# Where the low halves of weights are made: an adding DMA for the first weights of a sub-layer, VectorE for all 256-column chunks

## The chip, the cores and the metric

One core of one Trainium2 chip runs the whole program. The metric is the device time in microseconds (us) of one execution; lower is better. Engines are named as in the profile: PE is TensorE (matrix products, with PEld for its weight loads), DVE is VectorE, ACT is ScalarE, POOL is GpSimd, SP is SyncE, which here only issues DMA transfers.

## The reference

Two layers act on 512 latent tokens and 256 context tokens of width 1024, in float32. The even layer mixes by attention, the odd one by a short convolution; the context is dropped after the first layer's attention.

```python
def modulate(x, g, shift, scale):
    return rmsnorm(x, g) * (1 + scale) + shift

def swiglu(x, w_gate, w_up, w_down):
    return (jax.nn.silu(x @ w_gate) * (x @ w_up)) @ w_down

def macaron_ffn(xs, g, shift, scale, gate, w_gate, w_up, w_down):
    return xs + 0.5 * gate * swiglu(modulate(xs, g, shift, scale), w_gate, w_up, w_down)
...
    for i in range(DEPTH):
        ...
        x_lat = macaron_ffn(x_lat, norm_g[i, 0], m[0], m[1], m[2], ...)
        ...
        xn = modulate(x_lat, norm_g[i, 1], m[3], m[4])
        # even: xn @ w_in, neighbourhood and differential attention, @ w_out
        # odd:  xn @ w_in, three-tap convolution, @ w_out
        x_lat = x_lat + m[5] * y
        x_lat = macaron_ffn(x_lat, norm_g[i, 2], m[6], m[7], m[8], ...)
    return rmsnorm(x_lat, final_g)
```

## The kernel before

Each float32 product is made of three products of a shorter format: a weight is split into a high half `wh` and a low half `wl`, an activation into `xh` and `xl`, and `mm3` (L140) adds `wh·xh`, `wh·xl` and `wl·xh` in one accumulator. A weight tile is 128x1024 and serves as eight blocks of 128x128; a matmul streams 256 or 512 columns of tokens.

`load_w` (L109) fetches a weight tile into one of three `raw` buffers by a DMA of SP and splits it into one of three `wh` and one of three `wl` buffers. There are two ways. By default ScalarE copies `raw` to `wh` (L119) and VectorE subtracts (L120). Where `wl_eng[0]` is None, ScalarE writes `-raw` to `wl` (L115), a DMA issued by GpSimd adds `raw` to it (L116), and ScalarE writes `wh` (L117). Before the change only the projections inside attention go the second way: `wl_eng[0]` is set to None behind the first step of the projection stream and reset when the stream is done.

`modulate_chunk` (L287) makes one normalized chunk of 128 channels: a product on VectorE (L290), the high half with the shift on ScalarE (L296), the low half on VectorE (L297). Of chunks with up to 256 columns every third goes another way: ScalarE adds the shift (L292) and copies the high half (L293), and GpSimd subtracts (L294).

A sub-layer's first products are its head: `Head` loads three weights and runs them while the chunks of the first half of the tokens still come in. `transition` (L352) puts the last passes of the sub-layer before, the statistics (`Norm.add`: squares L271 on ScalarE, sums L275 on GpSimd or VectorE, then a matmul with ones, L284), the chunks and the head behind one another. There are five heads: to attention, to the FFN after it (f1), to layer two's first FFN (f2), to the convolution, and to the last FFN (f3). In attention, `proj_v` loads two weights for the first value projection: with the first four blocks of channels TensorE uses one, with the other four the other (L699); beside it the rope of queries and keys runs (shuffle L715, products L716 and L717, sum L718, copies L733 and L758).

The order on each engine is made by a scheduler from the order of the code and its own costs; it reorders instructions within an engine, and the engines wait for one another by semaphores. SP issues its DMAs in that order too, and a load whose buffer is still held keeps the ones behind it waiting.

Of the kernel before, what the change touches and what calls it, by code (L numbers as in the profile page):

```python
# [11 lines left out]
AF = mybir.ActivationFunctionType  # L12
ALU = mybir.AluOpType
# [28 lines left out]
def build(tc, A, out):  # L42

    nc = tc.nc
# [3 lines left out]
    with ExitStack() as es:  # L48
# [9 lines left out]
        def uid(s):  # L58
            cnt[0] += 1
            return f"{s}{cnt[0]}"  # L60
# [9 lines left out]
        def tt_(tag, shape=(P, NT), dtype=F32):  # L70
            return dp.tile(list(shape), dtype, tag=tag, bufs=BUFS[tag], name=uid(tag))

        def tmp(n):

            if n > 256:
                return dt_("pj")
            return dp.tile([P, 256], F32, tag="nh", bufs=BUFS["nh"], name=uid("nh"))
# [17 lines left out]
        wl_eng = [nc.vector]  # L95
# [13 lines left out]
        def load_w(src, n=1024, eng=None):  # L109
            raw = wp.tile([P, 1024], F32, tag="raw", bufs=3, name=uid("raw"))  # L110
            nc.sync.dma_start(raw[:, :n], src)
            hi = wp.tile([P, 1024], F32R, tag="wh", bufs=3, name=uid("wh"))
            lo = wp.tile([P, 1024], F32R, tag="wl", bufs=3, name=uid("wl"))
            if wl_eng[0] is None:
                nc.scalar.activation(lo[:, :n], raw[:, :n], AF.Copy, scale=-1.0)  # L115
                nc.gpsimd.dma_start(lo[:, :n], raw[:, :n], accum_op=ALU.add)  # L116
                nc.scalar.activation(hi[:, :n], raw[:, :n], AF.Copy)  # L117
                return hi, lo
            nc.scalar.activation(hi[:, :n], raw[:, :n], AF.Copy)  # L119
            (eng or wl_eng[0]).tensor_tensor(lo[:, :n], raw[:, :n], hi[:, :n], op=ALU.subtract)  # L120
            return hi, lo
# [135 lines left out]
        class Norm:  # L257


            def __init__(self, n):  # L260
                self.n, self.ss, self.k = n, [None, None], 0
                self.parts = 8
# [24 lines left out]
        def modulate_chunk(k, xk, y, s, b, hi, lo):  # L287
            n = xk.shape[-1]
            t = tmp(n)
            nc.vector.scalar_tensor_tensor(t[:, :n], xk, s[:, k:k + 1], y, op0=ALU.mult, op1=ALU.mult)  # L290
            if n <= 256 and k % 3 == 2:
                nc.scalar.activation(t[:, :n], t[:, :n], AF.Identity, bias=b[:, k:k + 1])  # L292
                nc.scalar.activation(hi, t[:, :n], AF.Copy)  # L293
                nc.gpsimd.tensor_tensor(lo, t[:, :n], hi, op=ALU.subtract)  # L294
                return
            nc.scalar.activation(hi, t[:, :n], AF.Identity, bias=b[:, k:k + 1])  # L296
            nc.vector.scalar_tensor_tensor(lo, t[:, :n], b[:, k:k + 1], hi, op0=ALU.add, op1=ALU.subtract)  # L297

# [5 lines left out]
        class Entry:  # L304
# [12 lines left out]
            def chunks(self, si, ks=range(KD)):  # L317
                l, i, ms, mb = self.key
                s0, s1 = self.segs[si]
                st = "c_ctx" if s0 >= N else "c"  # L320
                if st not in self.s:
                    need(l, ms)
                    need(l, mb)
                    self.s[st] = mod_scale(l, ms, i, st)
                for k in ks:
                    if self.xn[k] is None:
                        self.xn[k] = (tt_("xn", dtype=F32R), tt_("xn", dtype=F32R))
                    hi, lo = self.xn[k]
                    modulate_chunk(k, xseg(k, (s0, s1)), self.y[si], self.s[st], mod[l, mb, st],
                                   hi[:, s0:s1], lo[:, s0:s1])  # L330

        class Head:
# [2 lines left out]

            def __init__(self, units):

                self.w = [load_w(u[0]) for u in units]
                self.units = units

            def run(self, e, si, ks=range(KD), inner=False):
# [400 lines left out]
        def q_out(key, o):  # L742
            q = ((dt_("pj", dtype=F32R), dt_("pj", dtype=F32R)), dt_("pj", dtype=F32R))
            if key[0] == "d":
                q_parts(q, rope(o, 0.125), lambda z: z, None)
            else:
                ends = lambda z: z.rearrange("p (a b) -> p a b", b=64)
                q_parts(q, ends(o)[:, 0:8:7, :], lambda z: ends(z[:, 0:P]), 0.125)
                q_parts(q, o[:, 64:448], lambda z: z[:, P:N], 0.125)
            Q[key] = q  # L750
# [307 lines left out]
        def advance():  # L1058
            try:
                pos[1] += next(stream)  # L1060
            except StopIteration:
                return False
            return True

        advance()
        wl_eng[0] = None
        q_out(("d", 0), head0.o[0][0])
        for o, z in zip(head0.o[1], (SEG_LAT, SEG_CTX)):
            k_out(("d", 0), o, z)
# [24 lines left out]
        for j in range(4):  # L1094
            hi, lo = tt_("xn", dtype=F32R), tt_("xn", dtype=F32R)
# [171 lines left out]
```

## Time and profile before

| | |
|---|---|
| median of 3 runs | 2279.23 us (2277.51 to 2285.79) |
| profiled execution | 2278.66 us, span 2276.8 us |
| PE busy | 2210.0 us, 97% of the span |
| DVE busy | 1350.6 us, 59% |
| ACT busy | 890.5 us, 39% |
| POOL busy | 244.0 us, 11% |
| low halves by VectorE (L120) | 331 |
| low halves by DMA (L116) | 23 |

A row of a group in the profile names line, engine, operation, what is written and read (buffer numbers left out), the shape, the count; then busy time and mean ns of one; then the idle time of the engine just before them and what ended it. A row of the timeline gives start and length in us, the engine, the line, and in square brackets the idle time before it with its cause. In a row of waits stand the total, the count and the longest, in us.

### The profile page before, as it was taken

How to read it: one execution, taken by the hardware profiler on the slowest of the kernel's cores; microseconds unless marked ns; L12 is line 12 of the kernel's file. 1: busy time of each engine (PE TensorE's matmuls, PEld its weight loads, DVE VectorE, ACT ScalarE, POOL GpSimd, SP SyncE). 2: the span in 40 equal slices, each digit the busy share in tenths (PEclk: the TensorE clock that was granted, in tenths of full speed). 3: DMA queues.
4: the chain of work that ended last, by engine and by line, in shares of the span. 5: the costliest groups of instructions: out<-in, count | busy, mean ns of one | idle time of the engine just before them, and what ended most of it. 6: DMA issues, size and time to landing. Idle time of an engine off the chain costs nothing.

```text
span 2276.8 us, 30529 instructions
## 1 busy us (share of the span) xinstructions
PE 2210.0 (97%) x11728; PEld 1880.5 (83%) x11728; DVE 1350.6 (59%) x2388; ACT 890.5 (39%) x1512; POOL 244.0 (11%) x196
## 2 busy tenths in 40 slices
PE   5899999999999999999999999999999999999998
PEld 3688888888888888788888898888888889888887
DVE  8894763534787866775556476555437446443335
ACT  4651431212467887652222253222234224222224
POOL 3551520000221100020000010000001000000001
PEclk9989999999999999999999999999999999999999
DMA  7672443434533434334445444544332322223232
GB/s 240 220 238 83 149 139 107 149 106 130 162 86 77 102 74 113 111 100 159 152 163 178 152 143 157 167 162 159 96 102 93 101 93 92 94 97 98 86 109 74
DMA packets 113306, 291.14 MB, mean 128 GB/s; under 512 B 14468, under 2 KB 18820, under 8 KB 113160
## 3 DMA queue, kind: packets, MB, share of 16 engines
q1 hardware_dynamic: 109848, 277.13, 37.6%
q0 software_dynamic: 3312, 12.06, 2.8%
q8 instruction: 92, 1.51, 0.3%
q14 instruction: 54, 0.44, 0.1%
HBM read 272.88 MB, written 4.19 MB: 122 GB/s over the span
## 4 chain that ended last, share of the span: by engine, by line
PE 85%; DVE 8%; ACT 3%; issue 2%; DMA 1%; POOL 1%; SPq 0%; DVEq 0%; ACTq 0%; POOLq 0%
PE S L145 39%; PE acc L145 38%; PE acc L699 3%; DVE junk L215 1%; DVE wl L120 1%; PE S L768 1%; DVE xn L297 1%; PE S L766 1%; DVE sm L220 1%; DVE nh L290 1%; PE acc L978 1%; PE acc L893 1%; PE acc L1002 1%; POOL P L210 0%; PE acc L878 0%
## 5 line engine op out<-in xcount | busy, mean ns | idle before, releaser
L145 PE MATMUL S<-xn,wh 128*128 128x512 f32 (+1 forms) x3008 | 919.9, 379 | 20.7 <-ACT xn L296 12.7
L119 ACT ACTIVATE wh<-raw 128x1024 fp32r<-128x1024 f32 (+1 forms) x331 | 340.3, 1029 | 1049.9 <-PE acc L145 509.5
L145 PEld LDWEIGHTS S<-xn,wh 128*128 128x128 f32 x3008 | 555.4, 189 | 134.2 <-ACT xn L296 16.2
L120 DVE TENSOR_TENSOR wl<-raw,wh 128x1024 fp32r<-128x1024 f32 (+1 forms) x331 | 397.8, 1203 | 428.4 <-ACT wh L119 425.2
L145 PE MATMUL S<-xn,wl 128*128 128x512 f32 (+1 forms) x1504 | 568.6, 378 | 6.4 <-DVE wl L120 6.2
L145 PE MATMUL acc<-h,wh 128*128 128x512 f32 (+1 forms) x2148 | 531.9, 345 | 3.3 <-DVE x L475 3.2
L145 PE MATMUL acc<-xn,wh 128*128 128x256 f32 (+1 forms) x1664 | 447.7, 330 | 3.3 <-ACT wh L119 1.1
L145 PEld LDWEIGHTS acc<-h,wh 128*128 128x128 f32 x2148 | 363.0, 189 | 58.5 <-issue 3.3
L145 PE MATMUL acc<-h,wl 128*128 128x512 f32 (+1 forms) x1074 | 344.4, 343 | 1.4 <-DVE wl L120 1.4
L145 PEld LDWEIGHTS S<-xn,wl 128*128 128x128 f32 x1504 | 284.7, 189 | 61.0 <-DVE wl L120 8.5
L145 PEld LDWEIGHTS acc<-xn,wh 128*128 128x128 f32 x1664 | 295.3, 191 | 31.5 <-issue 2.5
L145 PE MATMUL acc<-xn,wl 128*128 128x256 f32 (+1 forms) x832 | 271.3, 326 | 2.9 <-DVE wl L120 2.9
L475 DVE SCALAR_TENSOR_TENSOR x<-acc,sm,x 128x512 f32<-128x512 f32 (+1 forms) x216 | 132.2, 629 | 217.2 <-PE acc L145 216.9
L145 PEld LDWEIGHTS acc<-h,wl 128*128 128x128 f32 x1074 | 192.4, 189 | 26.2 <-DVE wl L120 2.0
L215 DVE SCALAR_TENSOR_TENSOR junk<-aux,sc 128x512 bf16<-128x512 f32 x256 | 193.8, 757 | 1.6
L275 POOL TENSOR_TENSOR nh<-nh,nh 128x256 f32<-128x256 f32 x42 | 45.6, 1090 | 1232.9 <-ACT nh L271 898.5
L145 PEld LDWEIGHTS acc<-xn,wl 128*128 128x128 f32 x832 | 159.2, 191 | 16.1 <-DVE wl L120 3.6
L210 POOL TENSOR_TENSOR P<-aux,pv 128x512 f32<-128x512 f32 x64 | 103.4, 1630 | 132.3 <-ACT P L213 68.3
L126 ACT ACTIVATE h<-P 128x512 fp32r<-128x512 f32 (+2 forms) x99 | 62.5, 631 | 108.9 <-DVE P L434 108.8
L127 DVE TENSOR_TENSOR h<-P,h 128x512 fp32r<-128x512 f32 (+2 forms) x99 | 74.0, 747 | 20.1 <-ACT h L126 20.1
L699 PE MATMUL acc<-wh,xn 128*128 128x256 f32 x384 | 78.7, 294 | 0.0
L434 DVE TENSOR_TENSOR P<-P,S 128x512 f32<-128x512 f32 (+1 forms) x91 | 59.8, 657 | 10.4 <-ACT P L433 9.6
(179 smaller groups left out, 1741.8 us busy)
## 6 DMA issues: line engine op xcount, KB each, us to landing
aux<-modw SPq DMA_DIRECT2D x288, 256.0 KB
raw<-wu SPq DMA_DIRECT2D x92, 512.0 KB
raw<-wg SPq DMA_DIRECT2D x91, 512.0 KB
raw<-wd SPq DMA_DIRECT2D x59, 512.0 KB
raw<-wd SPq DMA_DIRECT2D x48, 384.0 KB
raw<-cin SPq DMA_DIRECT2D x24, 512.0 KB
wl<-raw POOLq DMA_DIRECT2D x23, 512.0 KB, 4.8
h<-modw SPq DMA_DIRECT2D x32, 256.0 KB
```

The lines of the kernel that those rows point to most:

```text
L119: nc.scalar.activation(hi[:, :n], raw[:, :n], AF.Copy)
L120: (eng or wl_eng[0]).tensor_tensor(lo[:, :n], raw[:, :n], hi[:, :n], op=ALU.subtract)
L126: nc.scalar.activation(hi, src, AF.Copy)
L127: nc.vector.tensor_tensor(lo, src, hi, op=ALU.subtract)
L145: last_mm[0] = nc.tensor.matmul(o, a, b[:, s0:s1], start=first and ti == 0, stop=last and ti == 2)
L210: nc.gpsimd.tensor_mul(pr, raw, sc[s][h])
L215: i = nc.vector.scalar_tensor_tensor(junk, raw, 1.0, sc[s][h], op0=ALU.mult, op1=ALU.mult, accum_out=a)
L220: nc.vector.scalar_tensor_tensor(o[:, ch:ch + 1], pt[:, 0:1], pt[:, 1:2], modb[:, c:c + 1], op0=ALU.add, op1=ALU.add)
L275: (nc.gpsimd, nc.vector)[i].tensor_add(self.ss[i][:, :n], self.ss[i][:, :n], sq[:, :n])
L434: nc.vector.tensor_mul(sl[:, s0:s1], sl[:, s0:s1], uu)
L475: nc.vector.scalar_tensor_tensor(v, ps, g[:, d:d + 1], v, op0=ALU.mult, op1=ALU.add)
L699: last_mm[0] = nc.tensor.matmul(o, a, b, start=k == 0 and ti == 0, stop=k == KD - 1 and ti == 2)
```

## The change

Weights of the five heads and both weights of the first value projection get their low halves by the adding DMA too (15 + 2 weights). The chunks with up to 256 columns lose their other way, so their 24 subtractions move from GpSimd to VectorE, and ScalarE does one instruction for each instead of two. Lines behind `Head` move by three: L699 becomes L696, L733 becomes L730, and so on; L290 stays, L296 becomes L291 and L297 becomes L292.

```diff
@@ modulate_chunk
             nc.vector.scalar_tensor_tensor(t[:, :n], xk, s[:, k:k + 1], y, op0=ALU.mult, op1=ALU.mult)
-            if n <= 256 and k % 3 == 2:
-                nc.scalar.activation(t[:, :n], t[:, :n], AF.Identity, bias=b[:, k:k + 1])
-                nc.scalar.activation(hi, t[:, :n], AF.Copy)
-                nc.gpsimd.tensor_tensor(lo, t[:, :n], hi, op=ALU.subtract)
-                return
             nc.scalar.activation(hi, t[:, :n], AF.Identity, bias=b[:, k:k + 1])
@@ Head.__init__
+                wl_eng[0] = None
                 self.w = [load_w(u[0]) for u in units]
+                wl_eng[0] = nc.vector
                 self.units = units
@@ attention
+        wl_eng[0] = None
         advance()
-        wl_eng[0] = None
         q_out(("d", 0), head0.o[0][0])
```

The scheduler's order changes around every head. At the f2 head, ScalarE before: `wh` of three weights in turn (L119), between them squares of the statistics (`nh`, L271) and chunks (`xn`, L296).

```order
L296 ACTIVATE xn_12748<-nh_12750,sm_10696 128x256 [waits DVE_49]
L119 ACTIVATE wh_12909<-raw_12907 128x1024 [waits DMAHW7_49,PE_49]
L271 ACTIVATE nh_12769<-x_9629 128x256 [waits DVE_49]
L271 ACTIVATE nh_12785<-x_9630 128x256 [waits DVE_49,Activation_49]
L296 ACTIVATE xn_12788<-nh_12790,sm_10696 128x256 [waits DVE_49]
L119 ACTIVATE wh_12915<-raw_12913 128x1024 [waits DMAHW2_49,PE_49]
L271 ACTIVATE nh_12809<-x_9627 128x256 [waits DVE_49,Pool_49]
L271 ACTIVATE nh_12824<-x_9628 128x256 [waits DVE_49,Activation_49]
L119 ACTIVATE wh_12921<-raw_12919 128x1024 [waits DMAHW3_49,PE_49]
```

And ScalarE now:

```order
L291 ACTIVATE xn_12744<-nh_12746,sm_10692 128x256 [waits DVE_49]
L117 ACTIVATE wh_12903<-raw_12901 128x1024 [waits DMAHW7_49,PE_49]
L271 ACTIVATE nh_12765<-x_9626 128x256 [waits DVE_49]
L271 ACTIVATE nh_12781<-x_9627 128x256 [waits DVE_49,Activation_49]
L115 ACTIVATE wl_12904<-raw_12901 128x1024 [waits DMASW4_49,PE_49]
L291 ACTIVATE xn_12784<-nh_12786,sm_10692 128x256 [waits DVE_49]
L271 ACTIVATE nh_12805<-x_9624 128x256 [waits DVE_49,Pool_49]
L115 ACTIVATE wl_12911<-raw_12908 128x1024 [waits DMAHW2_49,DMASW6_49,PE_49]
L271 ACTIVATE nh_12820<-x_9625 128x256 [waits DVE_49,Activation_49]
L117 ACTIVATE wh_12910<-raw_12908 128x1024
```

The first weight's negated copy stands two squares behind its high half; the second weight's stands ahead of its high half. On GpSimd, which had chunk subtractions (L294) behind the sums, the three adding DMAs now follow the sums:

```order
L275 TENSOR_TENSOR nh_12724<-nh_12724,nh_12739 128x256 [waits Activation_49]
L275 TENSOR_TENSOR nh_12724<-nh_12724,nh_12765 128x256 [waits Activation_49,Pool_49]
L275 TENSOR_TENSOR nh_12724<-nh_12724,nh_12781 128x256 [waits Activation_49,Pool_49]
L116 DMA wl_12904<-raw_12901 128x1024 [waits DMAHW7_49,DMASW4_49,Activation_49]
L116 DMA wl_12911<-raw_12908 128x1024 [waits DMAHW2_49,DMASW6_49,Activation_49]
L116 DMA wl_12918<-raw_12915 128x1024 [waits DMASW5_49,DMAHW3_49,DVE_49,Activation_49]
```

The sums read the squares of the two L271 rows above, so the first DMA stands behind both. TensorE at the same head, before:

```order
L145 MATMUL S_12905<-xn_12748,wh_12909 128x256 [waits Activation_49]
L145 MATMUL S_12905<-xn_12749,wh_12909 128x256
L145 MATMUL S_12905<-xn_12748,wl_12910 128x256 [waits DVE_49]
L145 MATMUL S_12905<-xn_12748,wh_12915 128x256 [waits Activation_49]
L145 MATMUL S_12905<-xn_12749,wh_12915 128x256
L145 MATMUL S_12905<-xn_12748,wl_12916 128x256 [waits DVE_49]
```

And now:

```order
L145 MATMUL S_12899<-xn_12744,wh_12903 128x256 [waits Activation_49]
L145 MATMUL S_12899<-xn_12745,wh_12903 128x256
L284 MATMUL acc_12958<-nh_12724,ones 128x256 [waits DVE_49,Pool_49]
L145 MATMUL S_12899<-xn_12744,wl_12904 128x256 [waits DMASW7_49]
L145 MATMUL S_12899<-xn_12744,wh_12910 128x256 [waits Activation_49]
L145 MATMUL S_12899<-xn_12745,wh_12910 128x256
L145 MATMUL S_12899<-xn_12744,wl_12911 128x256 [waits DMASW0_49]
```

One statistics matmul (L284) has moved ahead of the first matmul on a low half, and both low halves are awaited from the DMA (DMASW) instead of VectorE.

In the value projection, ScalarE before and now, from the rope's first copies out of the accumulators (L713, now L710); `raw_6007` and `raw_6003` are its second weight:

```order
L713 ACTIVATE x_6092<-acc_5677 128x512 [waits PE_49]
L119 ACTIVATE wh_6009<-raw_6007 128x1024 [waits DMAHW2_49,PE_49]
L733 ACTIVATE pj_6030<-x_6035 64x512 [waits DVE_49]
L733 ACTIVATE pj_6030<-x_6035 64x512
L758 ACTIVATE h_6046<-x_6050 64x512 [waits DVE_49]
```

```order
L710 ACTIVATE x_6089<-acc_5673 128x512 [waits PE_49]
L730 ACTIVATE pj_6027<-x_6032 64x512 [waits DVE_49]
L115 ACTIVATE wl_6006<-raw_6003 128x1024 [waits DMAHW7_49,DMASW1_49,PE_49]
L117 ACTIVATE wh_6005<-raw_6003 128x1024
L730 ACTIVATE pj_6027<-x_6032 64x512
```

The second weight's copies now stand behind a rope copy that waits for VectorE. On GpSimd its DMA stands behind the third rope product (L717, now L714):

```order
L116 DMA wl_5999<-raw_5996 128x1024 [waits DMAHW6_49,DMASW0_49,Activation_49]
L714 TENSOR_TENSOR x_6030<-x_6030,x_5992 128x512 [waits DMAHW4_49,DMAHW0_49,DVE_49]
L714 TENSOR_TENSOR x_6045<-x_6045,x_5992 128x512 [waits DMAHW5_49,DVE_49]
L714 TENSOR_TENSOR x_6089<-x_6089,x_5992 128x512 [waits DVE_49]
L116 DMA wl_6006<-raw_6003 128x1024 [waits DMAHW7_49,DMASW1_49,Activation_49]
```

TensorE now takes the first twelve matmuls of the second token tile, but for one on the second weight's high half, ahead of the first one on the second weight's low half.

## The prediction

> **What bounds the kernel now.** I read the busy times and the chain first, then who waits for the low halves, then the timeline at the places where the edit lands. From the profile page:
>
> ```profile
> PE 2210.0 (97%) x11728; PEld 1880.5 (83%) x11728; DVE 1350.6 (59%) x2388; ACT 890.5 (39%) x1512; POOL 244.0 (11%) x196
> ...
> q0 software_dynamic: 3312, 12.06, 2.8%
> ...
> PE 85%; DVE 8%; ACT 3%; issue 2%; DMA 1%; POOL 1%; SPq 0%; DVEq 0%; ACTq 0%; POOLq 0%
> ```
>
> TensorE is busy 97% of the span. Work taken from VectorE (59%) or GpSimd (11%) is worth only the TensorE waits that it ends, and any new wait of TensorE is paid in full, because TensorE has nothing else in its queue. So the question is narrow: at the five heads and at the first value projection, when does each low half `wl` come, and when does TensorE ask for it?
>
> The waits of TensorE inside the second head (to f1, 983.6 to 996 us) and inside the third (to f2, 1354.5 to 1363 us), with total, count and longest:
>
> ```profile
> PE S L145 <- POOL xn L294: 1.7, 1, 1.7
> PE S L145 <- DVE wl L120: 1.4, 1, 1.4
> ...
> PE S L145 <- DVE wl L120: 0.3, 1, 0.3
> PE S L145 <- POOL xn L294: 0.2, 1, 0.2
> ```
>
> The f1 head loses 3.1 us, the f2 head 0.5. The other three heads I take to be like f2, since they are built alike: about 5.1 us in all that the edit could at best give back there.
>
> **What each piece costs.** The groups of instructions that leave or multiply, and the low halves that already go by an adding DMA (23 of them, all in the attention layer; the last row is the time from issue to landing, minimum, median, maximum):
>
> ```profile
> L120 DVE TENSOR_TENSOR wl<-raw,wh 128x1024 fp32r<-128x1024 f32 x283 | 350.8, 1241 | 397.1 <-ACT wh L119 393.9 <-DMA xd<-x 0.5
> L297 DVE SCALAR_TENSOR_TENSOR xn<-nh,sm,xn 128x256 fp32r<-128x256 f32 x72 | 40.5, 578 | 1.5 <-ACT xn L296 1.5
> L294 POOL TENSOR_TENSOR xn<-nh,xn 128x256 fp32r<-128x256 f32 x24 | 29.8, 1245 | 88.4 <-ACT xn L293 80.5 <-DVE nh L290 8.0
> ...
> L115 ACT ACTIVATE wl<-raw x23: 1042/1058/1082, 653.9 to 926.4; 128x1024 fp32r<-128x1024 f32 x23
> L116 POOL DMA_DIRECT2D wl<-raw x23: 852/859/1007, 655.3 to 927.7; - x23
> ...
> DMA to landing us min/median/max: 4.5/4.8/6.6
> ```
>
> VectorE loses 17 subtractions of 1.24 us (21 us) and gains 24 of 0.58 us (14 us); GpSimd loses 24 of 1.25 us (30 us) and gains 17 issues of 0.86 us (15 us); ScalarE swaps 24 small copies for 17 negated copies of 1.06 us. None of the three is the bound, so these sums are worth nothing by themselves. What cover they have is slack beside TensorE, and at the 24 chunks it is worth at most the POOL waits above.
>
> What counts is latency. A low half made by VectorE is there 1.24 us after its high half. One made by DMA costs a negated copy (1.06), the hand-over to GpSimd (first copy 653.9 + 1.06, first issue 655.3: 0.3), and 4.8 to landing: 6.2 us from the copy's start, if nothing stands ahead of it. And transfers queue behind each other: q0 took 2.8% of 2276.8 us for 23 of them, 2.8 us each on all 16 engines, so two that are issued together land up to 2.8 us apart.
>
> **The f2 head, in full.** Its rows now, by start and length:
>
> ```profile
> 1348.92 1.06 ACT L119 ACTIVATE wh<-raw 128x1024 fp32r<-128x1024 f32 x1 [0.92 <-PE acc L145]
> 1349.90 0.87 ACT L271 ACTIVATE nh<-x 128x256 f32<-128x256 f32 x2
> 1352.72 1.04 ACT L119 ACTIVATE wh<-raw 128x1024 fp32r<-128x1024 f32 x1
> ...
> 1350.46 2.41 POOL L275 TENSOR_TENSOR nh<-nh,nh 128x256 f32<-128x256 f32 x2 [1.27 <-ACT nh L271]
> ...
> 1354.60 0.40 PE L145 MATMUL S<-xn,wh 128*128 128x256 f32 x2
> 1354.84 0.28 PE L145 MATMUL S<-xn,wl 128*128 128x256 f32 x1
> ```
>
> The first weight can be copied no sooner than 1348.92, when TensorE frees a buffer, and TensorE wants its low half at 1354.84: 5.9 us. In the new order ScalarE still makes the high half first, then two squares, then the negated copy at 1350.8. GpSimd is busy with the two statistics adds until 1352.87 and issues the DMA only then: landing 1357.7. TensorE meanwhile takes one statistics matmul forward (0.12 us, the pace of the two rows at 1354.60) and stands from 1354.96: **2.7 us**. The second weight's negated copy comes after one more square, 1353.1 to 1354.2, issue 1354.5, landing 1359.3 by itself or 1360.5 behind the first transfer. TensorE is there 0.36 us after the first landing, at 1358.0, so it stands 1.3 to 2.5; I take **2.0**. The third comes about when 22 further matmuls (2.6 us) are done: **0.3** (0 to 0.6). In all 5.0, where it waited 0.5.
>
> **The other heads, by the same steps** (to attention, to the convolution, to f1, to f3):
>
> ```profile
> 617.43 2.35 POOL L275 TENSOR_TENSOR nh<-nh,nh 128x256 f32<-128x256 f32 x2 [1.33 <-ACT nh L271]
> 621.81 0.28 PE L145 MATMUL S<-xn,wl 128*128 128x256 f32 x1
> ...
> 1716.28 2.31 POOL L275 TENSOR_TENSOR nh<-nh,nh 128x256 f32<-128x256 f32 x2 [1.37 <-ACT nh L271]
> 1720.69 0.28 PE L145 MATMUL acc<-xn,wl 128*128 128x256 f32 x1
> ...
> 980.37 1.54 POOL L275 TENSOR_TENSOR nh<-nh,nh 128x256 f32<-128x256 f32 x1 [1.49 <-ACT nh L271]
> 983.50 0.42 ACT L271 ACTIVATE nh<-x 128x256 f32<-128x256 f32 x1 [0.20 <-DVE x L1103]
> 983.93 0.28 PE L145 MATMUL S<-xn,wl 128*128 128x256 f32 x1
> ...
> 1894.31 1.06 ACT L119 ACTIVATE wh<-raw 128x1024 fp32r<-128x1024 f32 x1 [0.69 <-PE acc L145]
> 1895.28 0.40 ACT L271 ACTIVATE nh<-x 128x256 f32<-128x256 f32 x1
> 1897.19 1.06 ACT L119 ACTIVATE wh<-raw 128x1024 fp32r<-128x1024 f32 x1 [1.12 <-PE acc L145]
> ...
> 1900.23 0.28 PE L145 MATMUL S<-xn,wl 128*128 128x256 f32 x1
> ```
>
> - Attention: issue 619.8, landing 624.6, wanted 621.9: 2.7; second 2.0, as at f2.
> - Convolution: issue 1718.6, landing 1723.4, wanted 1720.7: 2.7. Nine matmuls (1.1 us) stand between its first two low halves instead of three, so the second costs 1.3.
> - f1: issue 981.9, landing 986.7, wanted 983.9: 2.8. The second negated copy stands behind the second high half and the square of 983.50, about 984.7 to 985.8: issue 986.1, landing 990.9, TensorE there at 987.4: 3.5.
> - f3: GpSimd is free; copy 1895.7 to 1896.7, issue 1897.0, landing 1901.8, wanted 1900.2: 1.6. The second copy follows the second high half (1897.19) and a square, 1898.7 to 1899.7, landing 1904.8, TensorE there at 1902.7: 2.1.
>
> First halves 12.5 us, second 10.9, third 5 times 0.3 = 1.5: 24.9, less the 5.1 of now, gives **+19.8**. With the shortest landing (4.5) and no queueing of transfers it is +13; with 6.6 for the first halves, +29.
>
> **The value projection.** Its two weights are used one after the other; the second is late now:
>
> ```profile
> 652.22 0.58 PE L699 MATMUL acc<-wl,xn 128*128 128x256 f32 x1 [3.64 <-DVE wl L120]
> 652.60 0.63 PE L699 MATMUL acc<-wh,xn 128*128 128x256 f32 x2
> 653.03 0.41 PE L699 MATMUL acc<-wl,xn 128*128 128x256 f32 x1
> ...
> 649.85 1.28 ACT L733 ACTIVATE pj<-x 64x512 fp32r<-64x512 f32 x2 [3.29 <-DVE x L718]
> ...
> 651.15 2.17 POOL L717 TENSOR_TENSOR x<-x,x 128x512 f32<-128x512 f32 x1 [2.48 <-DVE x L715]
> ```
>
> In the new order the first rope copy (L733, ready at 649.85) stands ahead of the second weight's two copies on ScalarE, and the third rope product (to 653.3) ahead of its DMA on GpSimd. With VectorE rid of one subtraction (1.2 us) the rope runs about that much earlier, so high half near 651.4, issue near 652.1, landing near 657. TensorE stands 2.8 us for the high half (from 648.6), does twelve matmuls of the next token tile that are moved forward (1.5 to 2.6 us), and stands 3 to 4 more: 6.2 against 3.64, **+2.5** (-1, if the rope runs 3 us earlier, to +5).
>
> **The clock.** Stalls also slow what follows. Columns: stretch, length, busy time of PE, PEld, DVE, ACT, POOL with counts, granted clock, DMA share, GB/s:
>
> ```profile
> 650.80:657.60 6.80, 5.38 (x25) 5.38 (x26) 6.67 (x10) 5.58 (x10) 3.17 (x2) 0.50 0.36 108
> 985.30:988.70 3.40, 1.76 (x11) 1.26 (x10) 3.40 (x7) 1.34 (x3) 0.00 (x0) 1.00 0.60 164
> 988.70:995.60 6.90, 5.19 (x22) 4.64 (x22) 5.59 (x15) 4.11 (x10) 3.29 (x2) 0.51 0.21 74
> ```
>
> In a stretch of 3.4 us TensorE worked 1.76, and got half the clock for the next 6.9. At half clock a matmul takes 0.215 (652.60 to 653.03 for two) instead of 0.12, so 3.4 us of it lose 1.5 us unless a wait lies there anyway. Each head will show some 5 us of waiting in 6 to 8. f1 and the value projection have their half clock already; for the four others I take half a window each, 4 times 0.75 = **+3** (0 to +12).
>
> By the Trainium skill, "TensorE: Matmul & The Clock Gate", Part 1, The HAM clock gate, the clock is halved after at least one idle window of some 3.4 us. Taken strictly, waits of 2 to 3 us would not halve it and the sum would lose its 3 us; the row at 985.30, half busy and followed by 0.51, disagrees, so I give that rule little weight. The Trainium skill, "DMA: Bandwidth & Descriptors", Anatomy of one DMA — SWDGE (gpsimd) path, fits such a transfer as 2.0 us plus bytes over 436e3; for 512 KB that gives an estimate of 3.2 us and five first halves 1.6 us earlier each, about 2296. The trace has 4.5 at best, so the sum stays with the trace.
>
> **What costs nothing.** SP's loads now wait for a raw buffer until the DMA has landed, some 6 us later than after the subtraction; a loaded weight feeds 24 matmuls of 0.12 us in the shortest use, and three buffers are in turn, so the next weights still have over 8 us. If that cover were gone, the fourth weight of a sub-layer would be late by up to 5 us.
>
> **The sum.** The profiled execution took 2278.66 us (span 2276.8 and 1.9 around it), 0.6 below the median 2279.23. 2278.7 + 19.8 + 2.5 + 3 = **2304**.
>
> **The rivals.**
> 1. Faster: the transfers are hidden, heads and value projection lose their waits (5.1 + 3.6) and their half clock (13.7 us of it, about 5): 2265. It decides at the f2 head if the DMA is issued by 1350.1, 4.8 us ahead of 1354.84 and the 0.12 moved forward. The high half alone runs until 1349.98, and the adds hold GpSimd until 1352.87. 4%.
> 2. Within 0.5%: only the first halves are waited for; the later transfers stream close behind, so second and third cost nothing: 2304 - 12.4 - 3 (shorter stalls, full clock) = 2288.6. For it: GpSimd can issue 0.86 us apart. Against: ScalarE makes the later copies that late. 12%.
> 3. The clock stays full through waits of 2 to 3 us, and the sum loses its 3: 2301. The row at 985.30 speaks against it. 14%.
> 4. The accumulating transfers land as slowly as the slowest now (6.6), because weights stream in at the heads, and each head pays one whole window of half clock: 1.8 for five first halves (+9) and 0.75 for four heads more (+3): 2316. 20%.
> My forecast, 50%: 2304, itself between 2294 and 2311.
>
> 0.5% (11.4 us) is about what a measurement of this kernel can tell from no change. Faster by more: rival 1, 4%. Within: rival 2, 12%. Slower: the rest, 84%. The range from 2288 to 2316 leaves out rival 1, about half of rival 2 and half of rival 4.
>
> **What would show it.** At each head the row of the first `wl` matmul carries 2 to 3 us of wait released by a DMA, the second one 1 to 3.5; POOL's issues stand right behind the L275 adds; landings are 4.5 to 6.6 us; the granted clock falls to about 0.5 behind at least two more heads; no wait on POOL `xn` is left. I am wrong if the first matmul on `wl` follows without a wait (the copies ran sooner than the order says), or if the second halves come with the first.

## Result and profile after

The changed kernel takes 2298.78 us (median of 6 runs, 2296.32 to 2308.46) against 2280.12 us (6 runs): the ratio is 1.0086, 95% interval 1.0069 to 1.0103. It is slower by some 0.9%, 19 us, where 2304 was forecast against 2279 (+25). Executions of one kernel can fall into two groups some 9 us apart (in one run below, 2276.6 to 2279.0 and 2285.8 to 2289.8), so the ratio counts for more than the difference of two medians, and profiles are compared place by place. The page of the changed kernel's profile:

```profile
span 2296.5 us, 30546 instructions
...
PE 2213.8 (96%) x11728; PEld 1886.9 (82%) x11728; DVE 1329.5 (58%) x2395; ACT 895.1 (39%) x1505; POOL 231.1 (10%) x189
...
q0 software_dynamic: 5760, 20.97, 5.0%
...
PE 85%; DVE 6%; ACT 3%; DMA 3%; issue 2%; POOL 0%; SPq 0%; DVEq 0%; ACTq 0%; POOLq 0%
```

VectorE is 21 us less busy and GpSimd 13, and neither was the bound. TensorE has the same 11728 matmuls, and the chain of work that ended last has a larger entry for DMA: 3% instead of 1%. The waits of TensorE (total, count, longest) name it:

```profile
PE S L145 <- DMA wl<-raw: 15.9, 10, 2.5
...
PE acc L145 <- DMA wl<-raw: 5.3, 4, 1.7
...
PE acc L696 <- DMA wl<-raw: 3.6, 1, 3.6
...
PE acc L696 <- ACT wh L117: 1.3, 1, 1.3
```

The first two rows are the five heads, 21.2 us; the last two are the value projection. No wait for GpSimd's `xn` is left. At the f2 head, ScalarE, GpSimd and TensorE now (start, length, what ended the idle time):

```profile
1354.44 1.06 ACT L117 ACTIVATE wh<-raw 128x1024 fp32r<-128x1024 f32 x1 [0.93 <-PE acc L145]
1355.42 0.87 ACT L271 ACTIVATE nh<-x 128x256 f32<-128x256 f32 x2
1356.19 1.04 ACT L115 ACTIVATE wl<-raw 128x1024 fp32r<-128x1024 f32 x1
...
1357.85 1.04 ACT L115 ACTIVATE wl<-raw 128x1024 fp32r<-128x1024 f32 x1
...
1355.98 1.61 POOL L275 TENSOR_TENSOR nh<-nh,nh 128x256 f32<-128x256 f32 x2 [1.28 <-ACT nh L271]
1357.53 0.88 POOL L116 DMA_DIRECT2D wl<-raw  x1
1359.19 0.86 POOL L116 DMA_DIRECT2D wl<-raw  x1 [0.78 <-ACT nh L271]
1362.09 0.86 POOL L116 DMA_DIRECT2D wl<-raw  x1 [2.04 <-DVE nh L290]
...
1360.12 0.40 PE L145 MATMUL S<-xn,wh 128*128 128x256 f32 x2
1360.36 0.59 PE L284 MATMUL acc<-nh,ones 128*128 128x256 f32 x2
1362.39 0.38 PE L145 MATMUL S<-xn,wl 128*128 128x256 f32 x1 [1.44 <-DMA wl<-raw]
...
1365.16 0.58 PE L145 MATMUL S<-xn,wl 128*128 128x256 f32 x1 [2.15 <-DMA wl<-raw]
```

The negated copy starts 3.9 us before TensorE begins the head, the DMA 2.6 us before, and it lands 2.2 us after that. Two stretches of this place, with the columns of the prediction's table:

```profile
1361.00:1364.40 3.40, 0.62 (x3) 0.41 (x3) 3.37 (x10) 3.40 (x7) 0.86 (x1) 0.94 1.04 186
1364.40:1367.80 3.40, 2.64 (x12) 2.64 (x13) 1.55 (x4) 0.65 (x2) 0.00 (x0) 0.50 0.92 219
```

TensorE works 0.62 us of 3.4, the mean busy share of the 16 DMA engines reads 1.04, and the next stretch has half the clock. Half clock comes at three heads that had none before: for 3.4 us at the head to attention, 6.8 at f2 and 3.4 at the convolution. f1 has 6.8 us of it, as before, and f3 none.

Setting the n-th matmul's end in both traces against each other shows where the time went:

| place | changed minus before, us |
|---|---|
| start to 200 us | -3.6 |
| 200 to 600 us | +0.3 |
| head to attention | +6.1 |
| value projection, to 900 us | +1.3 |
| 900 to 935 us (half clock for about one window) | +1.5 |
| f1 head | -0.1 |
| f2 head | +5.5 |
| convolution head | +4.4 |
| f3 head | +4.3 |
| sum | +19.7 |

For the experiments I use one measure beside the time: how long the 190 matmuls from each head's first one take, summed over the five heads, and how long TensorE is idle in them, each from the one profiled execution of a run. Before, this is 146.5 us with 5.6 idle; after, 166.6 with 21.2: 20.1 more, of which 15.6 is idle time and 4.5 slower matmuls.

### The profile page after: what moved, and what is told of

It is laid out like the page before. It is cut to its first block, busy times and chain, and to the rows that moved or that the text cites. A ratio compares the mean times of both kernels' runs of the same rounds, so it can differ in the third digit from the quotient of the medians.

```text
span 2296.5 us, 30546 instructions
## 1 busy us (share of the span) xinstructions
PE 2213.8 (96%) x11728; PEld 1886.9 (82%) x11728; DVE 1329.5 (58%) x2395; ACT 895.1 (39%) x1505; POOL 231.1 (10%) x189
## 4 chain that ended last, share of the span: by engine, by line
PE 85%; DVE 6%; ACT 3%; DMA 3%; issue 2%; POOL 0%; SPq 0%; DVEq 0%; ACTq 0%; POOLq 0%
PE S L145 39%; PE acc L145 38%; PE acc L696 3%; DMA wl<-raw 2%; DVE junk L215 1%; PE S L765 1%; DVE wl L120 1%; PE S L763 1%; PE acc L975 1%; PE acc L890 1%; DVE sm L220 1%; PE acc L999 1%; ACT wh L117 0%; DMA aux<-modw 0%; PE acc L875 0%
## 5 line engine op out<-in xcount | busy, mean ns | idle before, releaser
L119 ACT ACTIVATE wh<-raw 128x1024 fp32r<-128x1024 f32 (+1 forms) x314 | 322.4, 1027 | 1047.5 <-PE acc L145 496.2
L120 DVE TENSOR_TENSOR wl<-raw,wh 128x1024 fp32r<-128x1024 f32 (+1 forms) x314 | 379.0, 1209 | 434.9 <-ACT wh L119 432.2
L145 PEld LDWEIGHTS S<-xn,wl 128*128 128x128 f32 x1504 | 286.4, 190 | 77.7 <-DMA wl<-raw 19.6
L127 DVE TENSOR_TENSOR h<-P,h 128x512 fp32r<-128x512 f32 (+2 forms) x99 | 74.1, 749 | 19.8 <-ACT h L126 19.8
L696 PE MATMUL acc<-wh,xn 128*128 128x256 f32 x384 | 79.0, 294 | 1.3 <-ACT wh L117 1.3
L696 PEld LDWEIGHTS acc<-wh,xn 128*128 128x128 f32 x384 | 63.8, 196 | 4.0 <-issue 1.8
```

The costliest lines, as they stand in the source:

```text
L127: nc.vector.tensor_tensor(lo, src, hi, op=ALU.subtract)
L145: last_mm[0] = nc.tensor.matmul(o, a, b[:, s0:s1], start=first and ti == 0, stop=last and ti == 2)
L696: last_mm[0] = nc.tensor.matmul(o, a, b, start=k == 0 and ti == 0, stop=k == KD - 1 and ti == 2)
```

## The experiments

**The chunk edit alone.** Heads and value projection as before:

```diff
@@ Head.__init__ (against the changed kernel)
-                wl_eng[0] = None
                 self.w = [load_w(u[0]) for u in units]
-                wl_eng[0] = nc.vector
@@ attention
-        wl_eng[0] = None
         advance()
+        wl_eng[0] = None
```

> Only the chunk edit: all low halves of 256-column chunks on VectorE; heads and value projection as before. Theory A (the 3.6 us that the changed kernel is ahead at 180 us, and the small loss at f1, come from the chunks): 2 to 6 us faster than before (3 at the start, up to 2 at f1, where TensorE waited 1.7 us for a GpSimd subtraction): ratio 0.9975 to 0.999. Theory B (VectorE and GpSimd are off the path and the lead at the start is chance): within 1.5 us of before, and no lead at 180 us. Theory C (VectorE's 24 added instructions delay its subtractions of weights): slower by 2 us or more.

Measured: 2275.27 us, ratio 0.9972 (0.9957 to 0.9988). Faster by some 6 us, the upper end of theory A; with the first-weight run below it is the fastest version. In its profile the heads take 142.7 us, 3.4 idle: 2.5 us less at f1, 0.6 at f3, little at the others. 2.2 more are gained from 640 to 740 us, where the kernel before had 6.8 us of half clock behind the value projection and this one has none. The lead at the start is 1.2 us, not 3, so that part of theory A fell; the f1 part held.

**The heads alone.**

```diff
@@ modulate_chunk, attention: as before; of the change only
+                wl_eng[0] = None
                 self.w = [load_w(u[0]) for u in units]
+                wl_eng[0] = nc.vector
```

> Only the heads' 15 weights get low halves by the adding DMA; chunks and value projection as before. Theory A (latency at the heads is the loss): 19 to 24 us slower than before, 4 to 6 at each of the attention, f2, convolution and f3 heads and 0 to 3 at f1, with TensorE waiting for the DMA there. Theory B (it takes the chunk edit as well, because VectorE is what is late at the heads): under 12 us slower.

Measured: 2298.93 us against 2282.71, ratio 1.0058 (1.0042 to 1.0075), 13 us by the ratio. Heads 165.2 us, 18.8 idle, all of it waits for the DMA: +5.2, -0.4, +4.8, +4.7 and +4.3 over before, 18.7 in sum (13.2 over the same heads of the next run, which take 152.0). The DMA at the heads is the loss, place by place as theory A had it; the whole time is between the two theories' numbers.

**The value projection alone.**

```diff
@@ modulate_chunk, Head.__init__: as before; of the change only
+        wl_eng[0] = None
         advance()
-        wl_eng[0] = None
```

> Only the two weights of the first value projection get low halves by the adding DMA. Theory A: 1 to 3 us slower than before, all of it between 645 and 690 us, where TensorE waits 5 us or more instead of 3.6. Theory B (the order there is what costs, not the DMA; without the heads' DMAs ahead the scheduler puts it earlier): no change or up to 3 us faster.

Measured: ratio 1.0003 (0.9984 to 1.0022). The place itself costs 1.2 us in the profile (600 to 690 us), theory A's lower end; the time can't tell it from nothing. But the order there is not that of the changed kernel. The scheduler put the second weight earlier, as theory B supposed: ScalarE makes its copies ahead of the rope copies, its DMA goes out at 646.60 and lands 5.1 us later, and TensorE's one long wait, to 653.66, is for the rope's low half on VectorE (L759):

```profile
653.66 0.80 PE L766 MATMUL S<-h,pj 128*128 128x512 f32 x1 [5.16 <-DVE h L759]
```

So this run doesn't test the order that the changed kernel has at this place. It says something else: up to the projection its instructions stand in the same order as in the kernel before, and yet its profiled execution is 3.1 us ahead at 200 us. TensorE's longest wait there (for an eviction by VectorE, L475 in both) was 3.01 before and is 1.54 here:

```profile
174.97 1.03 PE L145 MATMUL acc<-h,wh 128*128 128x512 f32 x4 [1.54 <-DVE x L475]
```

Before, 3.4 us of half clock followed (176.37 to 179.78 us); here none did. So a lead of 3 us at the start is chance of an execution, and so may the changed kernel's -3.6 be.

Its heads are those of the kernel before, in the same order, and yet take 152.0 us instead of 146.5. TensorE waits longer for GpSimd's chunk subtractions; at the f2 head, where the kernel before waits 0.2 us for them (total, count, longest):

```profile
PE S L145 <- POOL xn L294: 1.5, 2, 1.3
```

So with the old chunk path the head measure differs by 5 us between these two profiled executions, and some of the chunk edit's gain is that this exposure goes. Without that path it holds still: 142.7 and 142.3 in the two runs (this section's first and the control below) whose heads are all VectorE's. The sums of the runs with the chunk edit are compared with these.

**Only the third weight of each head by DMA**, with the chunk edit:

```diff
-                wl_eng[0] = None
-                self.w = [load_w(u[0]) for u in units]
+                self.w = [load_w(u[0]) for u in units[:2]]
+                wl_eng[0] = None
+                self.w += [load_w(u[0]) for u in units[2:]]
                 wl_eng[0] = nc.vector
```

> Chunk edit kept; of each head only the third weight goes by the adding DMA, the first two by VectorE; value projection as before. Theory A (what costs is the 6 us of latency against a use 6 us away; the third weight is used 2.6 us later and so is covered): 0 to 2 us at each head, in all 4 us faster to 6 us slower than before. Theory B (the transfers disturb the heads themselves, by the DMA engines that they share with the weight loads or by the copies on ScalarE): a third to a half of the loss stays, 8 us slower or more.

Measured: ratio 0.9999 (0.9982 to 1.0016); heads 149.4 us, 6.7 more than with the chunk edit alone: 1.5 to 1.9 at four heads, nothing at f1. That is theory A's size, but theory A took the third weight for covered, and it is not: TensorE waits 0.9 to 1.5 us for its DMA at every head.

**Only the first weight by DMA**, with the chunk edit (the mirror of that diff, `units[:1]`):

> Chunk edit kept; of each head only the first weight goes by the adding DMA, the other two by VectorE; value projection as before. Theory A (each low half by DMA misses its own date by what latency and buffer release leave): 1.3 to 3 us slower at each of five heads than with the chunk edit alone, 2283 to 2290; its landings take 4.5 to 5 us, since no other adding DMA is in the queue. Theory B (one stall per head costs nearly as much as three, because the others hide behind it and behind half clock): 3.5 us or more at each head, 2292 or more.

Measured: 2277.08 us, ratio 0.9973 (0.9957 to 0.9990), as fast as with the chunk edit alone. TensorE does wait for the DMA, 1.2 to 2.1 us at each head (7.7 idle in sum, 4.4 more), but the heads take 143.0 us, only 0.3 more. Both theories asked too much. The four heads other than f1 take 2.4 us longer for 4.1 us more of idle time, so a wait at the very start of a head is not paid in full, as the forecast had it: at f2 0.6 us of later waits is gone, since the chunks and weights behind are then ready. f1 takes 2.1 us less, since it has no half clock here, where the chunk edit alone has 3.4 us of it.

**Only the second**, and **the first and the third**, with the chunk edit:

```diff
-                wl_eng[0] = None
-                self.w = [load_w(u[0]) for u in units]
+                self.w = []
+                for i, u in enumerate(units):
+                    wl_eng[0] = None if i == 1 else nc.vector   # the other run: i != 1
+                    self.w.append(load_w(u[0]))
+                wl_eng[0] = nc.vector
```

> Chunk edit kept; of each head only the second weight goes by the adding DMA. With the chunk edit alone the first 190 matmuls of the five heads take 142.7 us in sum, with only the first weight by DMA 143.0, only the third 149.4, all three 166.6. Theory A (each low half misses its own date, and the costs add up): the second alone costs what is left, 15 to 17 us in sum, time about 2290. Theory B (three adding DMAs in a row queue behind one another; alone the second lands in 4.5 to 5 us instead of 5.1 to 6.2): 3 to 9 us in sum, time 2277 to 2284.

> Chunk edit kept; of each head the first and the third weight go by the adding DMA, the second by VectorE. Theory A (costs add up): 7 us in sum more than the chunk edit alone, about 150 us for the first 190 matmuls of the five heads, time 2279 to 2286; the third lands 4.5 to 5 us after its issue, since the first is done by then. Theory B (the second transfer in a row is what makes the third late only if it is between them; two still disturb each other): 155 us or more in sum, and landings of 6 us and more for the third.

Measured: the second alone 2292.38 us, ratio 1.0037 (1.0019 to 1.0055), heads 154.7 us (+12.0); first and third 2297.23 us, ratio 1.0077 (1.0050 to 1.0103), heads 162.4 us (+19.7). The second alone lies between the theories, its landings 4.5 to 4.65 as theory B had them. Of its 11.0 us of idle time 6.5 are waits for the DMA and 3.3 waits for high halves that ScalarE copies (L119), so part of its cost is the extra copy on ScalarE and not the transfer. First and third together cost far more than 0.3 and 6.7: theory B there, and its third transfers land 5.9 to 8.2 us after issue though the first one is done. With the third alone at f2 (first block) and with first and third (second block), issue and landing of the adding DMAs there:

```profile
L116 POOL DMA_DIRECT2D wl<-raw x1: 877/877/877, 1362.0 to 1362.0; - x1
DMA to landing us min/median/max: 4.9/4.9/4.9
```

```profile
L116 POOL DMA_DIRECT2D wl<-raw x2: 859/863/867, 1354.6 to 1359.8; - x2
DMA to landing us min/median/max: 4.6/6.0/7.5
```

What runs beside them is seen in SP's own queue; first and third:

```profile
1351.15 0.33 SPq L111 DMA_DIRECT2D raw<-wg  x1
1359.17 0.33 SPq L111 DMA_DIRECT2D raw<-wu  x1
1359.67 0.33 SPq L111 DMA_DIRECT2D raw<-wg  x1
1367.39 0.33 SPq L111 DMA_DIRECT2D raw<-wu  x1
```

Third alone:

```profile
1352.33 0.33 SPq L111 DMA_DIRECT2D raw<-wg  x1
1355.13 0.33 SPq L111 DMA_DIRECT2D raw<-wu  x1
1358.76 0.33 SPq L111 DMA_DIRECT2D raw<-wg  x1
1367.01 0.33 SPq L111 DMA_DIRECT2D raw<-wu  x1
```

The first adding DMA holds its raw buffer until it lands, at 1359.12. SP's next load has been waiting for that buffer and starts 0.05 us later, the load behind it 0.5 us after, and the third adding DMA, issued at 1359.82, shares the engines with two loads of 512 KB: 7.5 us. Packets, MB and share of the 16 engines' time from its issue to its landing, for the loads (q1) and the adding DMA (q0):

```profile
q1 hardware_dynamic: 288, 1.05, 42.7%
q0 software_dynamic: 144, 0.52, 35.2%
```

With the third alone the loads went out in time, the last 3.2 us ahead of it, and q1 moves nothing until it lands: 4.9 us. The other heads of the first-and-third run agree. At the three heads with two loads beside it the third lands after 7.2 to 8.2 us, at the two with one load (f1, f3) after 5.9 and 6.1, and at none of them was another adding DMA in flight when it was issued.

All adding DMAs of the changed kernel, sorted by the loads issued from 1.5 us before to 3.5 us after them: none, 4.5 to 6.1 (median 4.6, 23 of them); one, 4.9 to 7.9 (12); two, 7.3 to 9.5 (5, one at each head, always the third). This sorting alone doesn't part loads from adding DMAs: 16 of the 17 with a load beside them were issued while an earlier adding DMA was in flight, and none of the 23 without one.

**A fourth buffer for low halves**, and its control with the chunk edit alone:

```diff
-                "x": 12, "sc": 2, "pj": 6, "pv": 4, "P1": 4, "aux": 4,
+                "x": 12, "sc": 2, "pj": 6, "pv": 4, "P1": 2, "aux": 4,
...
-            lo = wp.tile([P, 1024], F32R, tag="wl", bufs=3, name=uid("wl"))
+            lo = wp.tile([P, 1024], F32R, tag="wl", bufs=4, name=uid("wl"))
```

> The changed kernel with a fourth buffer for low halves (and two instead of four buffers of the tag P1, to make room). Theory A (a buffer comes free only 5.9, 3.5 and 3 us before TensorE wants the three low halves, and the route by DMA takes 6 us or more; that alone is the loss): each buffer is free one weight, 2.9 us, sooner, so the waits for the DMA at the five heads fall from 21 us in sum to under 8, and the heads cost 10 us or more less than in the changed kernel: 2280 to 2290. Theory B (the adding DMAs are slow at the heads because they share the DMA engines with the weight loads, whatever their start): the waits stay above 14 us and the time within 5 us of the changed kernel's.

> Control for the run with four buffers: only the chunk edit (heads and value projection on VectorE as before), with four buffers for low halves and two of the tag P1. Theory A: like the chunk edit alone, 2270 to 2280, since VectorE's low halves are not late enough to need the buffer. Theory B (the fourth buffer itself helps the heads, by 1 us at each): 2266 to 2272. If two P1 buffers cost something, it shows here in the attention layer.

Measured: 2302.59 us, ratio 1.0075 (1.0049 to 1.0102), and the control 2286.76 us, ratio 1.0032 (1.0013 to 1.0051). The control is some 11 us slower than the chunk edit alone with heads as short as there, so the buffer edits cost that much elsewhere, and it misses both its theories; that it is the two P1 buffers is likely, but no run has them alone. So the times can't be read against the changed kernel's; the heads can: 155.5 us with 14.4 idle, all of it waits for the DMA, against 142.3 in the control. The DMA costs 13.2 us at the heads instead of 23.9: about half the loss goes with the earlier start. The heads' time falls by 11.1, as theory A had it, but the waits stay where theory B had them (above 14, where A wanted under 8).

**High halves and sums out of the DMA's way**, on VectorE:

```diff
-                nc.scalar.activation(hi[:, :n], raw[:, :n], AF.Copy)
+                if hi_eng[0]:    # set while a head loads
+                    nc.vector.tensor_copy(hi[:, :n], raw[:, :n])
+                else:
+                    nc.scalar.activation(hi[:, :n], raw[:, :n], AF.Copy)
...
-                    (nc.gpsimd, nc.vector)[i].tensor_add(self.ss[i][:, :n], self.ss[i][:, :n], sq[:, :n])
+                    nc.vector.tensor_add(self.ss[i][:, :n], self.ss[i][:, :n], sq[:, :n])
```

> The changed kernel with the heads' high halves copied by VectorE instead of ScalarE, and the statistics' sums all on VectorE, so that neither a high half nor a sum stands ahead of the adding DMAs. Theory A (the release of the buffers sets the start): the first low half of a head comes in time, but the second and third still wait, about 3 us at each head instead of 4 to 5: 4 to 8 us faster than the changed kernel. Theory B (the order on ScalarE and GpSimd is the fault): the waits for the DMA all but vanish, 15 us or more faster than the changed kernel. Theory C: VectorE's added copies and sums are late themselves, no gain.

Measured: 2295.82 us, ratio 1.0057 (1.0036 to 1.0078) against the changed kernel's 1.0086 (1.0069 to 1.0103), intervals that overlap; heads 159.5 us, 7.1 less than in the changed kernel, 17.4 idle. Theory A's size, and mostly its mechanism: at f1, f2 and f3 the first low half is in time, at the other two heads TensorE still waits 1.7 and 0.6 us for it, and the second and third cost 13.5 us of waits. Clearing the way alone does not hide the transfers.

**A fourth raw buffer**, to part the loads from the adding DMAs:

```diff
-                "x": 12, "sc": 2, "pj": 6, "pv": 4, "P1": 4, "aux": 4,
+                "x": 12, "sc": 2, "pj": 6, "pv": 4, "P1": 2, "aux": 4,
...
-            raw = wp.tile([P, 1024], F32, tag="raw", bufs=3, name=uid("raw"))
+            raw = wp.tile([P, 1024], F32, tag="raw", bufs=4, name=uid("raw"))
```

> The changed kernel with a fourth raw buffer (and two instead of four buffers of the tag P1, which by the control costs some 11 us elsewhere). In the changed kernel each landing of an adding DMA frees a raw buffer, SP issues the next 512 KB load within 0.1 us, and that load runs beside the third adding DMA, which lands 7.3 to 9.5 us after issue. Theory A (that collision makes the third late): the loads come a weight earlier, the third lands in 6.5 us or less at most heads, and the first 190 matmuls of the five heads take 150 to 161 us instead of 166.6 (142.3 in the control). Theory B (the third is late because it queues behind the first and second adding DMA, whatever is loaded): it still lands in 7 us or more, and the heads stay within 4 us of 166.6.

Measured: 2309.03 us, ratio 1.0110 (1.0088 to 1.0131); heads 167.3 us; third landings 6.7 to 9.0, under 7 only at f1. Theory B's numbers, but its mechanism isn't tested: the loads did not move. SP runs ahead until all buffers are held, so with four buffers too, its loads go out right at the landings (at f2 1370.57 and 1373.73, behind landings at 1370.52 and 1373.67). The run doesn't part the theories; the first-and-third run does against B, since there no adding DMA was left in flight and the third still lands after 5.9 to 8.2 us. How much the second DMA, still in flight, adds to the 7.3 to 9.5 of the changed kernel stays open, and no run takes the loads away.

## Why the prediction was right

The mechanism came as forecast: TensorE waits for the DMA twice or three times at every head, and the clock falls behind it at three more heads. Step by step, forecast first:

- **First low halves: 12.5 us; measured 7.3** (1.3, 2.0, 1.4, 1.6, 1.1). The latency was right (landings 4.5 to 4.8), the issue was not: at f2 the two sums took 1.61 us, not the 2.41 of before, and the DMA went out 2.6 us ahead of the head, where I had 1.7; and the one statistics matmul ahead of the first `wl` runs as two records that take 0.59 us, where I had 0.12.
- **Second: 10.9; measured 9.7** (2.5, 1.5, 2.2, 1.7, 1.8). Landings 5.1 to 6.2.
- **Third: 1.5; measured 4.2** (1.5, 0.3, 0, 0.5, 1.9). This is the step that failed. I put the raw buffers' later release at nothing, because the loads have 8 us to spare. They have; but they go out at the landings of the first two DMAs, beside the third one, which lands after 7.3 to 9.5 us instead of 4.8 (with loads and no other adding DMA beside it, 5.9 to 8.2).
- **f1: +3.5; measured -0.1.** The second negated copy began 0.6 us ahead of TensorE's start of the head, where I had it 1.0 behind, and the wait for GpSimd's chunk is gone.
- **Clock: +3; slower matmuls made +4.5** in the heads, and 1.5 more at 924 us.
- **Value projection: +2.5; measured +1.3.** TensorE waits 1.28 for the high half and 3.59 for the DMA, against 3.64 before: the order worked as read, but TensorE came 2.8 us later, from the first head's stalls, and the rope copy did not (649.96, before 649.85).
- **Chunk edit: at most the waits for GpSimd's chunks, 1.7 us at f1 and 0.2 at f2; alone it is worth some 6**, 3.8 at the heads and 2.2 behind the value projection.
- **Start: 0; the profile has -3.3 by 600 us**, not the change's doing as far as the value projection's run tells.

By the Trainium skill, "TensorE: Matmul & The Clock Gate", Part 1, The HAM clock gate, the clock is halved after at least one idle window of some 3.4 us. Taken strictly, the trace disagrees, and it was right to give that rule little weight. The granted clock changes only at whole multiples of 3.41 us after its last change, so the clock's own windows can be cut. Three windows of the changed kernel at full clock, each with what followed it:

```profile
1360.59:1364.00 3.41, 0.98 (x5) 0.41 (x3) 3.38 (x10) 3.41 (x7) 0.86 (x1) 1.00 1.05 196
1364.00:1370.83 6.83, 5.67 (x23) 4.98 (x23) 1.95 (x5) 1.04 (x3) 0.00 (x0) 0.50 0.92 232
...
920.27:923.68 3.41, 2.17 (x12) 1.55 (x13) 3.33 (x7) 3.19 (x6) 0.06 (x1) 1.00 1.00 237
923.68:927.09 3.41, 3.41 (x10) 2.67 (x9) 3.38 (x8) 3.41 (x9) 0.00 (x0) 0.50 0.44 125
...
1916.96:1920.37 3.41, 1.66 (x10) 1.20 (x11) 3.17 (x9) 3.09 (x8) 0.86 (x1) 1.00 1.00 205
1920.37:1923.79 3.42, 3.14 (x25) 2.93 (x25) 3.42 (x10) 1.72 (x6) 0.00 (x0) 1.00 1.06 238
```

Half clock came behind 0.98 us of work at f2 and behind 2.17 at 924 us; at f3 the clock stayed full behind 1.66. The prediction's row at 985.30 is such a window too, to within 0.04 us, with half clock behind 1.76.

Rival 1 (hidden transfers) fell with the 21.2 us of waits, rival 2 (only the first halves) with the 9.7 and 4.2 for the second and third, rival 3 (full clock) with the half clock at three more heads. Rival 4's slow landings came, but for the third halves, not the first.

The forecast had 19.8 + 2.5 + 3 = 25.3. The profiles have 15.6 of added idle time at the heads, 4.5 and 1.5 of clock, 1.3 at the value projection and -3.3 at the start: 19.6. The sum was near in part by luck, because its misses had both signs: first halves and f1 too dear, third halves and the clock too cheap. The lower end that it gave for the heads, +13, does not come out of its steps, which make about +15 with 4.5 to landing, no queueing and no third wait.

## What to carry to other kernels

Before an operation is moved from an engine to a DMA, count the time from the release of its buffer to the first use: here 5.9 us for a route that takes 6.2, with 21 us of freed VectorE time worth nothing beside it. Here a DMA that reads a buffer holds it until it lands, and the load that waits for the buffer starts 0.05 us later, beside the next such DMA: look at what a later release lets loose, not only at whether it is in time. Try the parts of a change alone: here the part that took subtractions off GpSimd is 0.3% faster, the heads' part 0.6% slower.

## What the runs showed of the hardware

- What a stall costs depends on the clock behind it. With the first weight alone, 4.4 us of added idle time at the five heads cost 0.3 us, and no head has half clock (with the chunk edit alone f1 has 3.4 us of it). With the second alone, 7.6 us of added idle time cost 12.0, and three heads have half clock, 13.7 us in all.
- A window need not be idle to be followed by half clock. In the 13 profiles, cut on the clock's own windows of 3.41 us, all 80 windows at full clock in which TensorE worked less than 1.58 us were followed by half clock, 24 of the 144 with 1.58 to 2.33 us, and none with more.
- In five of the profiled executions all matmuls of the first FFN ran 1.9% slower, at a granted clock of 1.00 and with TensorE always busy. Columns as above; before, and with the first weight by DMA:

```profile
190.00:580.00 390.00, 390.00 (x2252) 341.05 (x2251) 201.22 (x387) 94.96 (x161) 44.71 (x28) 1.00 0.40 127
```

```profile
190.00:580.00 390.00, 390.00 (x2210) 338.06 (x2209) 197.59 (x381) 94.00 (x160) 46.14 (x28) 1.00 0.41 125
```

2210 matmuls instead of 2252 in 390 us make some 7.5 us by 580 us. The runs with the heads alone, the third, the second and the four buffers had it too; the changed kernel and the one before did not. It ends with that FFN, and what brings it on is open.
